# Second block of a two-block model: projections in a new order, sparse attention by pairs of heads, the memory maxima spread by one rounded product per head

## Chip, cores and metric

The kernel runs on one core of one Trainium2 chip. The metric is the device time of one execution in microseconds (us); the time before is the median of three runs, 1567.85 us (1567.51 to 1568.60).

## What is computed

512 tokens of width 1024 go through two different blocks, both in float32. The first block (differential attention, a convolution branch and a feed-forward part) is not touched. The second block is a mixer of three branches over one normalised input, followed by a convolutional feed-forward part:

```python
p = xn @ w_in
mq, mk, mv, mo, mi, mf, lx, lg, aq, ak, av, iq, ik, iw = split_cols(p)
hA = mlstm_chunkwise(mq, mk, mv, mi + b_igate, mf + b_fgate)   # 4 heads of 96
hA = rmsnorm(hA, mlstm_norm) * sigmoid(mo)
xc = causal_depthwise_conv(lx, lru_conv_w, lru_conv_b)
hB = rglru(xc, ...) * gelu(lg)                                 # width 384
hC = dsa_attention(aq, ak, av, iq, ik, iw)                     # 4 heads of 64
return concatenate([hA, hB, hC]) @ w_out
```

`dsa_attention` scores all keys by the index projections (`iq`, `ik`, `iw`), keeps the 128 best keys of each query, and runs a softmax attention of four heads of width 64 over them. `mlstm_chunkwise` is a linear attention whose weights are the exponential of a gate minus a running maximum over the tokens.

## The kernel before

Every large product takes its float32 operands as two rounded parts (type fp32r, high and low), and makes three products of them (high-high, high-low, low-high); `step` (L560) issues these three for one 128-row slice of the contraction, and `units` (L567) runs a unit: one block of 128 output columns over the 8 slices. Weights come in by DMA (`raw`), ACT rounds them (`wh`), and DVE makes the remainder (`wl`).

The order of all instructions is written by the program itself, while it is built: `Build` keeps an estimate of when each tile is ready, and the main thread issues one unit after another in the order of a table; after each `step` a tick (L200) lets background tasks (Python generators) issue what is due by that estimate. So PE's queue holds the units' products with small products of the tasks between them. On the chip every engine works off its own queue in order.

For the mixer of the second block (`block2_mix`, L1434) the table is `UNITS2` (L1355): 23 units that are the column blocks of `w_in`. `'f'` units write features by tokens, `'tok'` units (`av`, `t0`, `t1`, `t2`) tokens by features. `done` (L1795) and `done_tok` (L1837) copy a finished unit out of PSUM and set a flag with its name. `t0` and `t1` hold the values `va` of the memory heads, `t1` and `t2` their output gate `mo`; the last copy of `t2` is followed by two tanh on ACT over all of `mo`.

The tasks are:

- `gates` (L1454): the gates of the memory heads, and the running maximum `self.M` (4 rows, one for each head, by 512 tokens).
- `scores` (L1505): the index scores for the query tiles t = 1, 2, 3, and on DVE 16 rounds of 8 maxima for each tile (48 in all), then the mask `mbs`. They start when `iq1` is done. A score step issues the products of two heads, whose operands lie in partitions 0 to 63 and 64 to 127, behind each other.
- `lrus` (L1547): the recurrence branch, `hc[3]` to `hc[5]`.
- `memory` (L1604), one for each head: spreads the head's row of `self.M` to 128 partitions by a product with a column of the identity (contraction over 4 rows, float32), makes the weights, and sums the values. Two streams of `memories` (L1660) run the heads; they start when `t1` is done. Behind the last head follows one chain: squares on ACT, their sums on DVE, a reciprocal square root in small DVE operations on 16 columns, the scaling of both halves of the result and its product with `mo` on DVE, then on PE three times four transposes, each group read out by ACT and DVE into `hc[0]` to `hc[2]`.
- `sparse` (L1720), 16 steps (t, head): logits by a float32 product with a contraction over 64 rows, for t > 0 the mask added by a bf16 product, the maximum on DVE, the exponential on ACT, transposes on PE, a copy on ACT, the product with `av`, and the division on DVE. Three streams of `sparses` (L1764) run them. `sparse_out` (L1774) makes `hc[6]` and `hc[7]`.

After the table comes the product with `w_out` in 256-column halves. Its first unit (L1938) takes the eight `hc` in the order 3, 4, 5, 0, 1, 2, 6, 7, and goes through seven of them for the first block of columns before it starts the second block. A `hc` that is not there holds everything behind it on PE:

```python
for q, k in enumerate(order[: kt - 1] if len(outs_list) > 1 else order):
    if have:
        self.until(lambda: have(k))
    self.step(outs, ws[u], acts[k], k, q == 0, q == kt - 1)
```

Of the kernel before, what the change touches and what calls it, by code (L numbers as in the profile page):

```python
# [20 lines left out]
SEQ = 512  # L21
# [7 lines left out]
NEG = -1e30  # L29
# [133 lines left out]
class Build:  # L163
# [141 lines left out]
    def mm(self, out, lhsT, rhs, start=True, stop=True):  # L305
        n = free(rhs)
        if rhs.dtype == F32:
            c = max(0.213, n * 4 / 2400)
        elif rhs.dtype == F32R:
            c = max(0.107, n / 2400 + 0.003)  # L310
        else:
            c = max(0.03, n / 2400)
        self.pe_op(c, out, [lhsT, rhs])
        self.nc.tensor.matmul(out, lhsT, rhs, start=start, stop=stop)  # L314

    def tr(self, out, src):
# [922 lines left out]
    def block1_ffn(self):  # L1239
# [114 lines left out]

    UNITS2 = [  # L1355
        ('idx',),
        ('aq0', 'f', 2312),
        ('lg0', 'f', 1928),
        ('aq1', 'f', 2440),
        ('lx0', 'f', 1544),  # L1360
        ('lx1', 'f', 1672),
        ('lx2', 'f', 1800),
        ('iq0', 'f', 3080),
        ('mk0', 'f', 384),
        ('lg1', 'f', 2056),
        ('lg2', 'f', 2184),
        ('iq1', 'f', 3208),
        ('mk1', 'f', 512),
        ('av', 'tok', 2824),
        ('mk2', 'f', 640),  # L1370
        ('mq0', 'f', 0),
        ('mq1', 'f', 128),
        ('t0', 'tok', 768),
        ('mq2', 'f', 256),
        ('t1', 'tok', 1024),
        ('ak0', 'f', 2568),
        ('ak1', 'f', 2696),
        ('t2', 'tok', 1280),
    ]

# [53 lines left out]
    def block2_mix(self):  # L1434
        nc, tc, io, V, S, mm, tr = self.nc, self.tc, self.io, self.V, self.S, self.mm, self.tr
# [6 lines left out]
        with ExitStack() as es:  # L1442
# [3 lines left out]
            B = {}  # L1446
            flags = set()
            hc = [None] * 8
            gt = cst.tile([P, 4, 12], F32, name="gt")
            aa, em, nlf, pre, nF, fg = (g16(n) for n in ("aa", "em", "nlf", "pre", "nF", "fg"))  # L1450
            sp2, spm = cst.tile([P, 3], F32, name="sp2"), cst.tile([P, 3], F32, name="spm")
            wait = lambda f: (0.3 for _ in iter(lambda: f in flags, True))

            def gates():  # L1454
# [26 lines left out]
                for t in range(4):  # L1481
                    tr(pt[0:4, t * P : t * P + P], aa[:, 4 * t : 4 * t + 4])
                yield self.due(pt)
                self.M = B["gT"][0:4]
                V.tensor_copy(self.M, pt[0:4, 0:SEQ])
                self.at_put(i)
                V.tensor_tensor_scan(out=self.M, data0=self.M, data1=self.M, initial=0.0, op0=MAX, op1=MAX)
                yield self.due(self.M)
                i, pt = yield from self.at_get()
                for t in range(4):  # L1490
                    tr(pt[:, 4 * t : 4 * t + 4], self.M[:, t * P : t * P + P])
# [53 lines left out]
            lx = {}  # L1545
# [58 lines left out]
            def memory(h):  # L1604

                i, pt = yield from self.at_get()
                mm(pt[:, 0:512], self.ident[0:4, h : h + 1].to_broadcast([4, P]), self.M)
                yield self.due(pt)
                MB, MBm = halves(self.slot())
                S.activation(MB, pt[:, 0:512], AF.Copy)  # L1610
# [103 lines left out]
                    self.at_put(i)  # L1714
                    hc[c] = x

            STEPS = [(t, h) for t in range(4) for h in range(4)]
            osb, todo, ets = [], list(range(16)), []

            def sparse(n):  # L1720

                t, hd = STEPS[n]
                hp, r64 = hd // 2, slice(64 * (hd % 2), 64 * (hd % 2) + 64)
                yield from wait(f"aq{hp}")
                yield from wait(f"ak{hp}")
                if t:
                    yield from wait(f"mask{t}")
                L = P * (t + 1)
                yield self.due(B["aq"][hp], B["ak"][hp], self.mbs)
                i, pt = yield from self.at_get()  # L1730
                o = pt[:, :L]
                mm(o, B["aq"][hp][r64, t * P : t * P + P], B["ak"][hp][r64, :L], True, t == 0)
                if t:
                    mm(o, self.identb, self.mbs[:, 512 * (t - 1) : 512 * (t - 1) + L], False, True)
                yield self.due(pt)
                if t == 0:
                    V.memset(o[0:64, L - 64 :], NEG)
                nb, l, rl = (self.sm(1, x, bufs=5) for x in ("snb", "sll", "srl"))
                V.tensor_reduce(nb, o, axis=AX.X, op=MAX, negate=True)
                yield self.due(nb)  # L1740
                e = tp.tile([P, 3 + SEQ], F32, name=self.nm("e"), tag="lx", bufs=5)
                S.activation(e[:, :L], o, AF.Exp, bias=nb, accum_out=l)
                self.at_put(i)
                yield self.due(l, e[:, :L])
                i, pt = yield from self.at_get()
                for k in range(t + 1):
                    tr(pt[:, k * P : k * P + P], e[:, k * P : k * P + P])
                yield self.due(pt)
                while not ets:
                    yield 0.1  # L1750
                eT = ets.pop()
                S.activation(eT[:, :L], pt[:, :L], AF.Copy)
                self.at_put(i)
                V.reciprocal(rl, l)
                yield self.due(eT)
                i, pt = yield from self.at_get()
                for k in range(t + 1):
                    mm(pt[:, 0:64], eT[:, k * P : k * P + P], B["av"][:, k, 64 * hd : 64 * hd + 64], k == 0, k == t)
                ets.append(eT)
                yield self.due(pt)  # L1760
                V.tensor_scalar(osb[0][:, t, 64 * hd : 64 * hd + 64], pt[:, 0:64], rl, None, op0=MUL)
                self.at_put(i)

            def sparses():  # L1764
                yield from wait("av")
# [7 lines left out]

            def sparse_out():  # L1774
                for c in range(2):
                    for n in range(16):
                        if STEPS[n][1] // 2 == c:
# [12 lines left out]
                    hc[6 + c] = x  # L1790
# [416 lines left out]
```

## Time and profile before

| | |
|---|---|
| median of three runs | 1567.85 us (1567.51 to 1568.60) |
| the profiled execution, its own time | 1567.5 us |
| its span, first to last instruction | 1565.7 us |
| PE busy | 1546.3 us (99%), 10279 instructions |
| DVE busy | 1101.5 us (70%), 2011 instructions |
| ACT busy | 680.5 us (43%), 1222 instructions |
| mixer of the second block, its stretch of the span | about 928 to 1160 us |

PE multiplies, DVE and ACT work on vectors, POOL fills and gathers, SP issues the weights' DMAs. In a row of the timeline the first number is the start in us from the start of the span, the second the duration; consecutive matmuls overlap, so the cost of one is the distance to the next start (its step), not its duration. A float32 matmul stands as two records, since it is done in two passes. A note in square brackets is the idle time of the engine ahead of the row and what ended it. The granted clock is 1.00 for TensorE's level of 2.4 GHz and 0.50 for that of 1.2 GHz.

### The profile page before, as it was taken

Reading aid. Unit: us, or ns where it says so; the run is one execution under the profiler, and the core shown is the slowest. Engines: PE = TensorE matmul, PEld = TensorE weight load, DVE = VectorE, ACT = ScalarE, POOL = GpSimd, SP = SyncE. Lnnn points to the kernel's source line nnn. Section 1 sums busy time; section 2 is a strip of 40 time slices with the busy share of each in tenths; the row PEclk is TensorE's granted clock in tenths of the full one; section 3 lists DMA queues with packets and bytes.
Section 4 is the critical chain, followed back from the end, with each engine's and each line's share of the span. In section 5 each row is a group of like instructions: output and inputs, shape, how many; then the busy total and the mean of one; then the engine's idle time right before and its main releaser. Section 6 shows DMA issues by size and latency. Waiting matters only on the chain.

```text
span 1565.7 us, 25299 instructions
## 1 busy us (share of the span) xinstructions
PE 1546.3 (99%) x10279; PEld 1386.4 (89%) x10281; DVE 1101.5 (70%) x2011; ACT 680.5 (43%) x1222; POOL 25.9 (2%) x89
## 2 busy tenths in 40 slices
PE   7999999999999999999999999999999999999998
PEld 6999999999999999999988877796799888888886
DVE  4899999997764576776743457899768877775224
ACT  5344544546843343443432223625565544444112
POOL 4000000000000000000000000000000000000000
PEclk9999999999999999999999999999999999999999
DMA  5322222222222333333333332231053133333221
GB/s 145 95 69 75 75 70 80 68 68 68 73 77 71 92 108 93 85 94 95 91 88 98 84 99 80 59 104 55 19 144 109 55 95 95 95 98 102 94 95 68
DMA packets 233005, 134.17 MB, mean 86 GB/s; under 512 B 6925, under 2 KB 228240, under 8 KB 232888
## 3 DMA queue, kind: packets, MB, share of 16 engines
q1 hardware_dynamic: 231448, 130.35, 28.7%
q8 instruction: 81, 1.33, 0.4%
q0 software_dynamic: 1136, 1.15, 0.3%
q10 hardware_dynamic: 304, 1.05, 0.2%
q14 instruction: 36, 0.29, 0.1%
HBM read 130.44 MB, written 2.10 MB: 85 GB/s over the span
## 4 chain that ended last, share of the span: by engine, by line
PE 97%; DVE 1%; ACT 1%; DMA 0%; issue 0%; DVEq 0%; ACTq 0%; POOLq 0%
PE mm L314 70%; PE at L314 24%; PE at L320 3%; ACT act L158 1%; DVE act L158 0%; DMA act<-in_x_dram 0%; DVE yy L158 0%; DVE wl L158 0%; ACT ys L158 0%; DVE yc L158 0%; ACT wh L158 0%; DVE nb L158 0%; DVE fx L158 0%; DVE res L158 0%; ACT e L158 0%
## 5 line engine op out<-in xcount | busy, mean ns | idle before, releaser
L314 PE MATMUL mm<-act,wh 128*128 128x256 f32 (+3 forms) x4720 | 906.2, 306 | 1.5 <-DVE act L158 0.8
L314 PEld LDWEIGHTS mm<-act,wh 128*128 128x128 f32 (+1 forms) x4720 | 692.0, 189 | 49.5 <-issue 10.9
L314 PE MATMUL mm<-act,wl 128*128 128x256 f32 (+4 forms) x2360 | 562.8, 302 | 0.0
L158 ACT ACTIVATE wh<-raw 128x1024 fp32r<-128x1024 f32 (+2 forms) x235 | 245.7, 1047 | 367.5 <-PE mm L314 187.1
L158 DVE TENSOR_TENSOR wl<-raw,wh 128x1024 fp32r<-128x1024 f32 (+2 forms) x235 | 284.5, 1211 | 168.9 <-ACT wh L158 165.9
L314 PEld LDWEIGHTS mm<-act,wl 128*128 128x128 f32 (+1 forms) x2360 | 383.1, 189 | 18.0
L158 DVE SCALAR_TENSOR_TENSOR act<-u,par,act 128x514 f32<-128x514 f32 x232 | 161.1, 748 | 2.2 <-ACT act L158 2.2
L314 PE MATMUL at<-act,wh 128*128 128x512 f32 x416 | 130.3, 394 | 0.0
L314 PEld LDWEIGHTS at<-act,wh 128*128 128x128 f32 x416 | 78.1, 188 | 18.4
L314 PE MATMUL at<-wh,act 128*128 128x512 f32 x264 | 86.0, 395 | 0.0
L314 PE MATMUL mm<-wh,act 128*128 128x256 f32 (+1 forms) x344 | 84.4, 320 | 0.0
L314 PE MATMUL at<-act,act 128*128 128x256 f32 (+9 forms) x468 | 83.5, 329 | 0.8 <-ACT act L158 0.7
L314 PE MATMUL at<-act,wl 128*128 128x512 f32 x208 | 82.0, 394 | 0.0
L158 DVE TENSOR_TENSOR act<-act,act 128x514 f32<-128x514 f32 (+4 forms) x122 | 69.7, 589 | 8.2 <-ACT act L158 7.5
L314 PEld LDWEIGHTS at<-act,act 128*128 128x128 f32 (+1 forms) x468 | 60.2, 189 | 11.1 <-issue 4.7
L158 DVE SCALAR_TENSOR_TENSOR ft<-fx,par,ft 128x512 f32<-128x512 f32 x88 | 65.8, 749 | 1.5
L158 DVE TENSOR_TENSOR fx<-mm,rB 128x514 f32<-128x514 f32 x44 | 30.5, 694 | 50.3 <-PE mm L314 50.1
L314 PEld LDWEIGHTS mm<-wh,act 128*128 128x128 f32 x344 | 57.9, 189 | 7.3 <-issue 3.4
L158 ACT ACTIVATE act<-mm 128x528 f32<-128x528 f32 (+2 forms) x64 | 35.1, 548 | 66.8 <-PE mm L314 66.7
L158 ACT ACTIVATE act<-at 128x128 f32<-128x128 f32 (+6 forms) x88 | 34.4, 413 | 67.8 <-PE at L314 50.2
L158 DVE SCALAR_TENSOR_TENSOR gy<-gx,par,gy 128x512 f32<-128x512 f32 x84 | 62.6, 748 | 1.5
L314 PEld LDWEIGHTS at<-wh,act 128*128 128x128 f32 x264 | 49.6, 188 | 11.6
(286 smaller groups left out, 1435.8 us busy)
## 6 DMA issues: line engine op xcount, KB each, us to landing
raw<-in_w_in_dram SPq DMA_DIRECT2D x82, 512.0 KB, 3.8
raw<-in_w_up_dram SPq DMA_DIRECT2D x44, 512.0 KB, 3.8
raw<-in_ffn_up_dram SPq DMA_DIRECT2D x44, 512.0 KB, 3.9
raw<-in_ffn_down_dram SPq DMA_DIRECT2D x22, 512.0 KB, 3.2
raw<-in_w_out_dram SPq DMA_DIRECT2D x20, 512.0 KB, 3.8
raw<-in_w_down_dram SPq DMA_DIRECT2D x16, 512.0 KB, 3.8
raw<-in_w_conv_out_dram SPq DMA_DIRECT2D x8, 512.0 KB, 3.8
raw<-in_w_down_dram SPq DMA_DIRECT2D x8, 384.0 KB, 3.3
```

The lines of the kernel that those rows point to most:

```text
L158: return f(*a, **k)
L314: self.nc.tensor.matmul(out, lhsT, rhs, start=start, stop=stop)
L320: self.nc.tensor.transpose(out, src, self.ident[p0 : p0 + k, p0 : p0 + k])
```

## The change

Four edits:

1. `UNITS2` gets another order. `iq0` and `iq1` come right behind `idx`, the `mk` units come earlier, `ak0` and `ak1` move from behind `t1` to places ahead of `mq1` and `mq2`. Behind `t1` only `t2` is left, where before `ak0`, `ak1` and `t2` were.
2. `gates` also builds `self.ML`, a tile of 64 rows of type fp32r that is zero but for rows 0 to 3 (the rounded running maximum) and rows 32 to 35 (the remainder), and `self.sel`, which adds the two.
3. `memory` spreads its row by one fp32r product over these 64 rows in place of the float32 product over 4 rows.
4. A step of `sparse` takes two heads: both logits are issued behind each other, then both masks, and then the rest of each head in turn. There are 8 steps, and two streams in place of three.

```diff
     UNITS2 = [
         ('idx',),
+        ('iq0', 'f', 3080),
+        ('iq1', 'f', 3208),
         ('aq0', 'f', 2312),
-        ('lg0', 'f', 1928),
-        ('aq1', 'f', 2440),
         ('lx0', 'f', 1544),
         ('lx1', 'f', 1672),
         ('lx2', 'f', 1800),
-        ('iq0', 'f', 3080),
+        ('lg0', 'f', 1928),
         ('mk0', 'f', 384),
+        ('aq1', 'f', 2440),
+        ('mk1', 'f', 512),
         ('lg1', 'f', 2056),
+        ('mk2', 'f', 640),
         ('lg2', 'f', 2184),
-        ('iq1', 'f', 3208),
-        ('mk1', 'f', 512),
         ('av', 'tok', 2824),
-        ('mk2', 'f', 640),
         ('mq0', 'f', 0),
+        ('ak0', 'f', 2568),
         ('mq1', 'f', 128),
         ('t0', 'tok', 768),
+        ('ak1', 'f', 2696),
         ('mq2', 'f', 256),
         ('t1', 'tok', 1024),
-        ('ak0', 'f', 2568),
-        ('ak1', 'f', 2696),
         ('t2', 'tok', 1280),
     ]
...
+            self.sel = cst.tile([64, 4], F32R, name="sel")
...
-                self.M = B["gT"][0:4]
+                self.M, ML = B["gT"][0:4], self.slot(F32R)[0:64, 0, :SEQ]
+                zero = self.ident[0:64, None, :].to_broadcast([64, 4, P])
+                V.tensor_scalar(ML.rearrange("p (t n) -> p t n", n=P), zero, 0.0, None, op0=MUL)
+                V.tensor_tensor(self.sel, self.ident[0:64, 0:4], self.ident[0:64, 32:36], op=ADD)
...
                 yield self.due(self.M)
+                S.activation(ML[0:4], self.M, AF.Copy)
+                yield self.due(ML)
+                tt(ML[32:36], self.M, ML[0:4].bitcast(F32), SUB)
+                self.ML = ML
...
-                mm(pt[:, 0:512], self.ident[0:4, h : h + 1].to_broadcast([4, P]), self.M)
+                mm(pt[:, 0:512], self.sel[:, h : h + 1].to_broadcast([64, P]), self.ML)
...
-            STEPS = [(t, h) for t in range(4) for h in range(4)]
-            osb, todo, ets = [], list(range(16)), []
+            STEPS = [(t, hp) for t in range(4) for hp in range(2)]
+            osb, todo, ets = [], list(range(8)), []
...
-                i, pt = yield from self.at_get()
-                o = pt[:, :L]
-                mm(o, B["aq"][hp][r64, t * P : t * P + P], B["ak"][hp][r64, :L], True, t == 0)
+                ats = []
+                for _ in range(2):
+                    ats.append((yield from self.at_get()))
+                for q, (_, pt) in enumerate(ats):
+                    r64 = slice(64 * q, 64 * q + 64)
+                    mm(pt[:, :L], B["aq"][hp][r64, t * P : t * P + P], B["ak"][hp][r64, :L], True, t == 0)
                 if t:
-                    mm(o, self.identb, self.mbs[:, 512 * (t - 1) : 512 * (t - 1) + L], False, True)
+                    for _, pt in ats:
+                        mm(pt[:, :L], self.identb, self.mbs[:, 512 * (t - 1) : 512 * (t - 1) + L], False, True)
...
-            for _ in range(3):
+            for _ in range(2):
                 self.start(sparses(), 0.0)
```

Since the tasks issue their work where it is due, the whole mixer is issued in another order. Three places follow.

PE, the last query tile of the sparse attention (t = 3; `at` are its PSUM tiles, `act_1313` and `act_1174` the queries and keys of two heads, `sel` the selector of the memory heads). Before, one head with its mask:

```order
L314 MATMUL at_1521_11936<-act_1369_11334,act_1173_10107 128x512
L314 LDWEIGHTS identb_114
L314 MATMUL at_1521_11936<-mbs_9890,identb_114 128x512
L314 MATMUL at_1522_11939<-act_1259_10631,act_1277_10762 128x64 x4
L314 MATMUL at_1523_11944<-act_1259_10631,act_1277_10762 128x64 x4
```

Now:

```order
L314 MATMUL at_1481_11703<-act_1211_10300,sel_9882 128x512
L314 MATMUL at_1482_11705<-act_1313_10932,act_1174_10111 128x512
L314 MATMUL at_1483_11706<-act_1313_10932,act_1174_10111 128x512
L314 LDWEIGHTS identb_114
L314 MATMUL at_1482_11705<-mbs_9891,identb_114 128x512
L314 LDWEIGHTS identb_114
L314 MATMUL at_1483_11706<-mbs_9891,identb_114 128x512
```

The two heads' logits stand behind each other, and the product that spreads a memory maximum reads `sel`. In the order of before, logits from different halves of the partitions are neighbours at two places among the 16: two heads of t = 0, and a head of t = 0 with one of t = 1.

PE, from the last product of the last unit `t2` to the transposes of the memory branch (`at<-ident`, from the finished halves of the result), and on. Before (`mm_1395` is `t2`, `mm_1510` the first block of `w_out`, `e_` the exponentials of the sparse attention, `act_1515` and `act_1518` the halves):

```order
L314 MATMUL mm_1395_11436<-wh_1372_11342,act_1142_9857 128x256
L320 MATMUL at_1506_11879<-ident_109,e_1501_11865 128x128 x3
L314 MATMUL mm_1510_11889<-act_1266_10700,wh_1397_11442 128x256 x2
L314 MATMUL mm_1510_11889<-act_1266_10700,wl_1398_11443 128x256
L320 MATMUL at_1516_11904<-ident_109,e_1505_11874 128x128 x4
L314 MATMUL mm_1510_11889<-act_1279_10769,wh_1397_11442 128x256 x2
L314 MATMUL mm_1510_11889<-act_1279_10769,wl_1398_11443 128x256
L314 MATMUL mm_1510_11889<-act_1287_10810,wh_1397_11442 128x256 x2
L314 MATMUL mm_1510_11889<-act_1287_10810,wl_1398_11443 128x256
L314 MATMUL at_1519_11924<-act_1259_10631,act_1277_10762 128x64 x3
L320 MATMUL at_1520_11928<-ident_109,e_1517_11909 128x128 x4
```

The first transposes of the halves (`at_1527`) stand 6 rows behind these, and more sparse work stands behind them. Now (`mm_1451` is `t2`, `mm_1530` the first block of `w_out`, `act_1543` and `act_1544` the halves, `act_1546` is `hc[0]`):

```order
L314 MATMUL mm_1451_11551<-wh_1453_11554,act_1142_9857 128x256
L314 MATMUL mm_1530_11959<-act_1285_10755,wh_1464_11583 128x256 x2
L314 MATMUL mm_1530_11959<-act_1285_10755,wl_1465_11584 128x256
L314 MATMUL mm_1530_11959<-act_1287_10784,wh_1464_11583 128x256 x2
L314 MATMUL mm_1530_11959<-act_1287_10784,wl_1465_11584 128x256
L314 MATMUL mm_1530_11959<-act_1290_10819,wh_1464_11583 128x256 x2
L314 MATMUL mm_1530_11959<-act_1290_10819,wl_1465_11584 128x256
L320 MATMUL at_1545_12021<-ident_109,act_1543_12012 128x128 x2
L320 MATMUL at_1545_12021<-ident_109,act_1544_12016 128x128 x2
L320 MATMUL at_1547_12029<-ident_109,act_1543_12012 128x128 x2
L320 MATMUL at_1547_12029<-ident_109,act_1544_12016 128x128 x2
L314 MATMUL mm_1530_11959<-act_1546_12026,wh_1464_11583 128x256 x2
```

All of the sparse attention stands ahead of the end of `t2`; between that end and the transposes there are the nine products of `hc[3]` to `hc[5]`.

ACT, the same place. Now, from the copy of the last memory head's sums (`at_1522`) on (`mm_1451` is the last copy of `t2`, `act_1277` and `act_1479` are `mo`, `act_1535` and `act_1536` the squares):

```order
L158 ACTIVATE act_1455_11556<-at_1522_11901 128x2x97
L158 ACTIVATE act_1456_11557<-at_1522_11901 128x2x97
L158 ACTIVATE act_1479_11667<-mm_1451_11551,R_9868 128x256
L158 ACTIVATE act_1277_10697<-act_1277_10697 128x512
L158 ACTIVATE act_1479_11667<-act_1479_11667 128x1024
L158 ACTIVATE act_1535_11972<-act_1455_11556 128x768
L158 ACTIVATE wh_1533_11966<-raw_1452_11552 128x1024
L158 ACTIVATE act_1536_11983<-act_1456_11557 128x768
L158 ACTIVATE wh_1538_11988<-raw_1463_11581 128x1024
L158 ACTIVATE act_1546_12026<-at_1545_12021,wn_9918 128x512
```

Before, the two squares stood 7 and 4 rows ahead of the last copy of `t2`, with the tanh behind it; now they stand behind both. On DVE, the remainder `wl` of the second `w_out` unit stands between the sums of the first and the second square.

## Rows read from the trace of the kernel before

**Rows 1.** The page, busy time of each engine.
```profile
PE 1546.3 (99%) x10279; PEld 1386.4 (89%) x10281; DVE 1101.5 (70%) x2011; ACT 680.5 (43%) x1222; POOL 25.9 (2%) x89
```

**Rows 2.** Busy us of PE, PEld, DVE, ACT, POOL in the mixer's last stretch.
```profile
1124.50:1143.50 19.00, 17.51 (x132) 14.87 (x131) 11.91 (x25) 12.12 (x24) 0.20 (x2) 1.00 0.20 56
```

**Rows 3.** Timeline of PE, the last wait of that stretch.
```profile
1143.50 0.50 PE L314 MATMUL mm<-act,wh 128*128 128x256 f32 x2 [0.48 <-ACT act L158]
```

**Rows 4.** Timeline of PE: index scores, then logits; start, duration, operation, records.
```profile
1007.87 1.13 PE L314 MATMUL at<-act,act 64*128 64x512 f32 x4
1008.93 0.39 PE L314 MATMUL mm<-wh,act 128*128 128x256 f32 x1
...
1084.45 0.70 PE L314 MATMUL at<-act,act 64*128 64x128 f32 x4
...
1121.83 0.28 PE L314 MATMUL mm<-wh,act 128*128 128x256 f32 x1
1122.04 1.12 PE L314 MATMUL at<-act,act 64*128 64x512 f32 x2
1123.10 0.39 PE L314 MATMUL at<-mbs,identb 128*128 128x512 bf16 x1
...
1123.91 0.40 PE L314 MATMUL mm<-wh,act 128*128 128x256 f32 x2
```

**Rows 5.** Timeline of PE: the spreading of one memory head's maximum.
```profile
1085.72 1.12 PE L314 MATMUL at<-act,ident 4*128 4x512 f32 x2
1086.77 0.39 PE L314 MATMUL mm<-wh,act 128*128 128x256 f32 x1
```

**Rows 6.** Groups of PE by shape, 928 to 1160 us: busy us, mean ns of one.
```profile
L314 PE MATMUL mm<-act,wl 128*128 128x512 f32 x120 | 47.3, 394 | 0.0
```

**Rows 7.** Timeline of PE, the last product of `t2`, and of ACT around it.
```profile
1124.27 0.28 PE L314 MATMUL mm<-wh,act 128*128 128x256 f32 x1
...
1116.35 0.84 ACT L158 ACTIVATE act<-act 128x768 f32<-128x768 f32 x1
...
1124.59 0.47 ACT L158 ACTIVATE act<-mm,R 128x256 f32<-128x256 f32 x1 [0.97 <-PE mm L314]
1124.96 1.57 ACT L158 ACTIVATE act<-act 128x512 f32<-128x512 f32 x2
...
1129.36 1.08 ACT L158 ACTIVATE wh<-raw 128x1024 fp32r<-128x1024 f32 x1
1131.88 0.69 ACT L158 ACTIVATE act<-at,wn 128x512 fp32r<-128x512 f32 x1 [1.43 <-PE at L320]
```

**Rows 8.** Timeline of DVE, the memory branch's chain.
```profile
1117.22 0.95 DVE L158 TENSOR_REDUCE sumsq<-act 128x8 f32<-128x768 f32 x1
1118.09 0.17 DVE L158 TENSOR_TENSOR den<-den,em 128x16 f32<-128x16 f32 x1
...
1121.51 0.17 DVE L158 TENSOR_TENSOR rd<-rd,rsy 128x16 f32<-128x16 f32 x1
...
1127.25 0.94 DVE L158 TENSOR_TENSOR act<-act,rd 128x768 f32<-128x768 f32 x1
1128.22 1.03 DVE L158 SCALAR_TENSOR_TENSOR act<-act,act 128x256 f32<-128x256 f32 x2
...
1129.49 1.21 DVE L158 TENSOR_TENSOR wl<-raw,wh 128x1024 fp32r<-128x1024 f32 x1
...
1132.77 0.74 DVE L158 SCALAR_TENSOR_TENSOR act<-at,wn,act 128x512 fp32r<-128x512 f32 x1
```

**Rows 9.** Timeline of PE near both ends, and the last window's granted clock (before DMA share).
```profile
5.40 1.09 PE L320 MATMUL mm<-ident,act 128*128 128x128 f32 x4 [2.56 <-DMA act<-in_x_dram]
...
24.36 0.76 PE L320 MATMUL at<-ident,act 128*128 128x128 f32 x5
...
1558.53 0.39 PE L314 MATMUL mm<-wh,act 128*128 128x512 f32 x1
...
1564.00:1566.00 2.00, 0.00 (x0) 0.00 (x0) 0.00 (x0) 0.00 (x0) 0.00 (x0) 0.50 0.16 59
```

More of the change, by code (lines that the diff above doesn't have):

```diff
@@ L1715, in memories @@
                     hc[c] = x
-            STEPS = [(t, h) for t in range(4) for h in range(4)]
-            osb, todo, ets = [], list(range(16)), []
+            STEPS = [(t, hp) for t in range(4) for hp in range(2)]
+            osb, todo, ets = [], list(range(8)), []
             def sparse(n):
-                t, hd = STEPS[n]
-                hp, r64 = hd // 2, slice(64 * (hd % 2), 64 * (hd % 2) + 64)
+                t, hp = STEPS[n]
                 yield from wait(f"aq{hp}")
@@ L1729, in sparse @@
                 yield self.due(B["aq"][hp], B["ak"][hp], self.mbs)
-                i, pt = yield from self.at_get()
-                o = pt[:, :L]
-                mm(o, B["aq"][hp][r64, t * P : t * P + P], B["ak"][hp][r64, :L], True, t == 0)
-                if t:
-                    mm(o, self.identb, self.mbs[:, 512 * (t - 1) : 512 * (t - 1) + L], False, True)
[L1735 to L1762, printed above, removed]
+                ats = []
[4 more added lines that the diff above has]
+                    mm(pt[:, :L], B["aq"][hp][r64, t * P : t * P + P], B["ak"][hp][r64, :L], True, t == 0)
@@ new lines, in sparse @@
+                if t:
+                    for _, pt in ats:
+                        mm(pt[:, :L], self.identb, self.mbs[:, 512 * (t - 1) : 512 * (t - 1) + L], False, True)
+                es = []
+                for i, pt in ats:
+                    o = pt[:, :L]
+                    yield self.due(pt)
+                    if t == 0:
+                        V.memset(o[0:64, L - 64 :], NEG)
+                    nb, l = (self.sm(1, x, bufs=5) for x in ("snb", "sll"))
+                    V.tensor_reduce(nb, o, axis=AX.X, op=MAX, negate=True)
+                    yield self.due(nb)
+                    e = tp.tile([P, 3 + SEQ], F32, name=self.nm("e"), tag="lx", bufs=5)
+                    S.activation(e[:, :L], o, AF.Exp, bias=nb, accum_out=l)
+                    self.at_put(i)
+                    es.append((e, l))
@@ new lines, in sparse @@
+                for q, (e, l) in enumerate(es):
+                    hd, rl = 2 * hp + q, self.sm(1, "srl", bufs=5)
+                    yield self.due(l, e[:, :L])
+                    i, pt = yield from self.at_get()
+                    for k in range(t + 1):
+                        tr(pt[:, k * P : k * P + P], e[:, k * P : k * P + P])
+                    yield self.due(pt)
+                    while not ets:
+                        yield 0.1
+                    eT = ets.pop()
+                    S.activation(eT[:, :L], pt[:, :L], AF.Copy)
+                    self.at_put(i)
+                    V.reciprocal(rl, l)
+                    yield self.due(eT)
+                    i, pt = yield from self.at_get()
+                    for k in range(t + 1):
+                        mm(pt[:, 0:64], eT[:, k * P : k * P + P], B["av"][:, k, 64 * hd : 64 * hd + 64], k == 0, k == t)
+                    ets.append(eT)
+                    yield self.due(pt)
+                    V.tensor_scalar(osb[0][:, t, 64 * hd : 64 * hd + 64], pt[:, 0:64], rl, None, op0=MUL)
+                    self.at_put(i)
@@ L1775, in sparse_out @@
                 for c in range(2):
-                    for n in range(16):
-                        if STEPS[n][1] // 2 == c:
+                    for n in range(8):
+                        if STEPS[n][1] == c:
                             yield from wait(f"sp{n}")
```

## The prediction

> **What bounds the kernel now.** I read the page's busy times first: PE is busy for 1546.3 of 1565.7 us [rows 1], so what the change takes off PE's queue or adds to PE's waits is the time, and the other engines matter only where PE waits for them. The second view is the table of stretches: in the mixer's last 19.00 us PE is busy for 17.51, so it waits 1.49 us there [rows 2]; one wait of 0.48 us is for the copies of the first `w_out` block [rows 3], which stays. Ahead of that stretch the mixer's PE waits next to nothing. Third comes the timeline of PE, for what each small product costs: its step to the next start. Last come the timelines of ACT and DVE around the end of the unit `t2`, because the new order leaves something uncovered there.
>
> **Logits by pairs.** The index scores already show what a pair costs: two heads at 512 columns, four records, start at 1007.87, and the next product at 1008.93, 1.06 us for both [rows 4]. One head alone takes 1.06 us as well (1122.04 to 1123.10). So the second head is free, since the two use different halves of the partitions. A step is some 0.06 below the duration: 0.64 us at 256 columns (1084.45, where a head of t = 0 rides along), and midway, 0.85, at 384. Before, t = 1, 2, 3 each pay four times; now twice. That is 2 x (0.64 + 0.85 + 1.06) = 5.1 us. For t = 0 nothing changes: one pair, one rider and one alone before, two pairs now. Entering a 64-row product costs extra: the product ahead of it takes 0.21 us (1121.83 to 1122.04), where 0.12 is usual (0.40 for two less 0.28 for one) [rows 4]. Fourteen entries become eight: 0.5 us. Together **-5.6 us**; ends -4.5 (no entry saved, pairs a little apart) and -6.
>
> **Spreading the maxima.** Four products of 1.05 us each (1085.72 to 1086.77) [rows 5], in two float32 passes. One fp32r pass of 512 columns has a mean duration of 0.394 us [rows 6], a step of 0.23. The new product also enters and leaves a 64-row form, so its cost lies between 0.23 and half of the old one, 0.53; I take 0.33, near the row of its own type. 4 x 0.72 = **-2.9 us**; ends -2.1 and -3.3. Building `ML` and `sel` adds three DVE instructions and one on ACT in the chain of the gates, well ahead of its first reader (which waits for `t1`); PE has units to do there, so I cost it at nothing. If that cover were gone it would be about 2 us, four operations at about the 0.47 to 0.69 us of ACT rows of this size [rows 7].
>
> **The order itself** adds or removes no large product and no DMA; each queue has the same transfers. Scores and rounds of maxima come earlier, so all of the sparse attention ends ahead of `t2`'s end. The small waits in the last stretch go with it: 1.49 - 0.48 = **-1.0 us**. Up to here the gains are 9.5 us.
>
> **What is late next: the chain of the memory branch.** It starts when `t1` is done. Before, `ak0`, `ak1`, `t2` and half of the sparse attention lay behind that; now only `t2` does. Between the end of `t2` and the transposes of the halves PE's queue holds nine products, 9 x 0.12 = 1.1 us, and PE works in order. Count from the end of `t2`'s last product, z = 1124.27 + 0.28 in the trace of before [rows 7].
>
> ACT: the copy starts at z + 0.04 (1124.59) and the tanh at z + 0.41 (1124.96); they end at z + 2.0, and the first square, now queued behind them, runs from about z + 1.9 to 2.75 (0.84). A rounding of weights follows (1.08, to 3.75), and then the second square, to 4.5 [rows 7]. DVE: the sum of the first square, then the remainder `wl` (1.21), which waits for the rounding and ends at z + 4.9; behind it the second sum, step 0.87 (1117.22 to 1118.09), to 5.8 [rows 8]. The small operations step through 3.4 us (1118.09 to 1121.51) and 0.2 for the last: z + 9.4. Each half of the result takes 2.0 us (1127.25 to the end of 1128.22 + 1.03): z + 11.4 and **z + 13.3**.
>
> PE restarts there. The first group's last two transposes need 0.2, and 0.3 to come out; ACT takes 0.69 (the row at 1131.88) and DVE 0.74 (1132.77): `hc[0]` is whole at z + 15.3, `hc[1]` by DVE's queue at 15.9, and `hc[2]`, whose transposes stand behind the products of `hc[0]`, at 17.6. With its last products PE is through at z + 17.8. The work done in that time, 18 products at 0.12 and 12 transposes at 0.11, is 3.4 us, begun 0.2 us ahead of z. So PE loses 17.8 + 0.2 - 3.4 = **+14.6 us**. Ends: 12 if the remainder `wl` doesn't delay the second sum and the transposes of the first half start the rest early; 17 if the last head's copies are late as well.
>
> **The clock.** After PE's last product at 1558.53 the granted clock is 0.50, the 1.2 GHz level, in the window 1564 to 1566 [rows 9]; the new gap, from z + 0.9 to z + 11.4, is 10.5 us, longer than that. At the program's start four transposes take 1.09 us, 0.22 apart; at 24.36 five take 0.76, 0.12 apart [rows 9]. At the slow step the transposes and products of the restart add 1.2 us to the chain above, and I let six more products pass slowly, 0.7 us: **+1.9 us**, a choice, since no row here shows a gap in mid-program; ends 0 and 3.
>
> The Trainium skill (TensorE: Matmul & The Clock Gate, section "Why this matters for your kernels") warns of idle gaps between bursts of matmuls in mid-kernel, because TensorE goes back to half its clock. It speaks against this change, which buys fewer PE cycles with a gap; rows 9 agree for the program's end. By the rule the sum is the one below, without it 1.9 us less.
>
> **Sum.** The profiled execution took 1567.5 us. 1567.5 - 5.6 - 2.9 - 1.0 + 14.6 + 1.9 = 1574.5. The median of the three runs lies 0.35 us above the profiled one, so I forecast 1574.9 us, 0.45% slower.
>
> **Rivals.** A measurement of this kernel can tell a difference of about 0.2%, 3.1 us, from none.
>
> 1. *Faster: the chain is covered.* PE saves its 9.5 us and the gap doesn't open: 1567.85 - 9.5 = 1558.4. For it: PE's share of 99% [rows 1], so whatever PE saves shows at once; and before, the same chain cost PE next to nothing. The point that decides: the time from `t2`'s end to the halves, which has to stay below the 1.1 us of products queued there; with a loss under 9.5 - 3.1 = 6.4 us it would still be measurably faster. Against: the two squares stand behind the tanh in ACT's order, and 5.8 us of DVE's and ACT's rows lie between them and the small operations alone. Chance 0.11.
> 2. *Half of it.* If DVE and ACT go through the tail faster than before's rows, a loss of 6.4 to 12.6 us and no slow clock leaves the time within 0.2%: 1564.7 to 1571.0. Chance 0.09.
> 3. *The clock stays up*: 1573.0. For it: 10.5 us is not far above what rows 9 show. Chance 0.14.
> 4. *A starved middle.* Index scores and 48 rounds come earlier, where DVE must also make each unit's `wl` of 1.21 us; PE would wait at unit starts, 1 to 4 us more: 1576 to 1579. Against: DVE has 30% free over the span [rows 1]. Chance 0.10.
> 5. *The change doesn't do what it says on PE*: masks or PSUM keep the pair's products apart, or the fp32r product over 64 rows costs what the old one did; 8.5 us of the gain are lost at most, about 1580. Against: the pairs of the index scores. Chance 0.05.
>
> **How the numbers follow.** The forecast, 1573.5 to 1576.5, gets 0.51. Slower by over 0.2% are the forecast and rivals 3, 4 and 5: 0.51 + 0.14 + 0.10 + 0.05 = 0.80. Within 0.2% is rival 2, 0.09; faster is rival 1, 0.11. The range for 8 in 10 goes from 1569.7 (gains whole, the loss 12 us and no slow clock, 1567.85 - 10.2 + 12) to 1578.8 (gains 7.5, loss 15.5, clock 3: 1567.85 + 11); it takes in the forecast, rival 3, most of rival 4 and the upper part of rival 2, and leaves out rivals 1 and 5.
>
> **What would show it.** In the profile after: two logits of equal length starting within 0.01 us of each other, 1.06 us for a pair at 512 columns; the spreading product as one record with a step near 0.33; PE's busy time down by some 9 us; a new wait of PE for DVE of about 10 us near 1130 to 1140, with the transposes of the halves behind it; the tanh ahead of the squares on ACT; and a granted clock of 0.50 somewhere behind that gap. I am wrong if PE shows no wait of over 5 us there, or if the squares or the last copy of the memory heads turn out to be done well ahead of `t2`.

## The result, and the profile after

| | before | after |
|---|---|---|
| median | 1568.22 us (1567.51 to 1569.81, 4 runs) | 1577.26 us (1576.52 to 1577.71, 4 runs) |
| span of the profiled execution | 1565.7 us | 1575.3 us |

The ratio is 1.0056, interval 1.0040 to 1.0072: 0.56% slower, where 0.45% was forecast. (Of all the runs in this document one execution, 4180.94 us in the last experiment, stands apart from its ten neighbours and is left out of the ratio there.) PE's busy time shrank all the same, by 3.3 us. The page's busy times of after, against [rows 1]:

```profile
PE 1543.0 (98%) x10276; PEld 1387.1 (88%) x10277; DVE 1100.1 (70%) x2014; ACT 680.9 (43%) x1223; POOL 25.8 (2%) x89
```

What became of the logits and of the spreading stands in the groups of PE by shape from 928 to 1180 us (busy us, mean ns of one). Before (index scores of the same shapes are in the groups, alike in both kernels):

```profile
L314 PE MATMUL at<-act,act 64*128 64x512 f32 x16 | 6.7, 641 | 0.0
L314 PE MATMUL at<-act,act 64*128 64x384 f32 x16 | 5.5, 535 | 0.0
L314 PE MATMUL at<-act,ident 4*128 4x512 f32 x8 | 4.5, 639 | 0.0
L314 PE MATMUL at<-act,act 64*128 64x256 f32 x16 | 4.2, 428 | 0.0
L314 PE MATMUL at<-act,act 64*128 64x128 f32 x8 | 1.5, 322 | 0.0
```

After:

```profile
L314 PE MATMUL at<-act,act 64*128 64x512 f32 x16 | 4.7, 634 | 0.1
L314 PE MATMUL at<-act,act 64*128 64x384 f32 x16 | 3.7, 535 | 0.0
L314 PE MATMUL at<-act,act 64*128 64x256 f32 x16 | 2.8, 428 | 0.0
L314 PE MATMUL at<-act,sel 64*128 64x512 f32 x4 | 2.0, 495 | 0.0
L314 PE MATMUL at<-act,act 64*128 64x128 f32 x8 | 1.0, 323 | 0.0
```

The logits' numbers of records are the same, and the mean of one is nearly so, but busy time counts what overlaps once: the logits fall from 17.9 to 12.2 us, by 5.7, and the spreading from 4.5 to 2.0, by 2.5. Now the other side, the two largest of PE's waits of after (us in total, times, longest) in the same stretch:

```profile
PE at L320 <- DVE act L158: 11.0, 2, 9.7
PE mm L314 <- DVE act L158: 1.5, 3, 0.9
```

The 9.7 us are the gap behind `t2`. PE's timeline of after around it:

```profile
1127.95 0.28 PE L314 MATMUL mm<-wh,act 128*128 128x256 f32 x1
...
1129.02 0.28 PE L314 MATMUL mm<-act,wl 128*128 128x256 f32 x1
1139.01 0.69 PE L320 MATMUL at<-ident,act 128*128 128x128 f32 x2 [9.71 <-DVE act L158]
1140.94 1.54 PE L320 MATMUL at<-ident,act 128*128 128x128 f32 x6 [1.24 <-DVE act L158]
...
1143.34 0.58 PE L314 MATMUL mm<-act,wh 128*128 128x256 f32 x1 [0.35 <-DVE act L158]
...
1146.56 0.58 PE L314 MATMUL mm<-act,wh 128*128 128x256 f32 x1 [0.20 <-DVE act L158]
...
1152.65 0.51 PE L314 MATMUL mm<-act,wh 128*128 128x256 f32 x2 [0.48 <-ACT act L158]
```

The first row is the last product of `t2`, so z = 1127.95 + 0.28 = 1128.23; then come the nine products of `hc[3]` to `hc[5]`, nothing for 9.7 us, and the transposes of the first half. The chain that they wait for, on ACT and DVE of after (compare [rows 7, 8]):

```profile
1128.64 2.29 ACT L158 ACTIVATE act<-act 128x512 f32<-128x512 f32 x3
```

```profile
1131.91 1.22 DVE L158 TENSOR_TENSOR wl<-raw,wh 128x1024 fp32r<-128x1024 f32 x1
1133.06 0.95 DVE L158 TENSOR_REDUCE sumsq<-act 128x8 f32<-128x768 f32 x1
...
1137.33 0.17 DVE L158 TENSOR_TENSOR rd<-rd,rsy 128x16 f32<-128x16 f32 x1
1137.54 0.96 DVE L158 TENSOR_TENSOR act<-act,rd 128x768 f32<-128x768 f32 x1
...
1140.46 1.03 DVE L158 SCALAR_TENSOR_TENSOR act<-act,act 128x256 f32<-128x256 f32 x2
```

The two tanh and the first square are one row of three on ACT; the remainder `wl` stands ahead of the second sum on DVE; the small operations end at z + 9.3 and the second half at 1141.49, z + 13.3. The granted clock by stretches of after (start and end, length, the busy us of PE, PEld, DVE, ACT and POOL, then the clock as the third number from the end):

```profile
1130.00:1135.00 5.00, 0.00 (x0) 0.00 (x0) 3.89 (x9) 3.56 (x5) 0.00 (x0) 0.80 0.09 24
...
1145.00:1150.00 5.00, 4.66 (x20) 4.07 (x20) 0.75 (x1) 0.69 (x1) 0.00 (x0) 0.50 0.15 44
1150.00:1155.00 5.00, 4.51 (x37) 4.31 (x37) 0.78 (x1) 3.15 (x6) 0.00 (x0) 0.99 0.00 0
```

It falls to the 1.2 GHz level (0.50) within the gap and is still there from 1145 to 1150, where PE has its products again; it is back in the stretch from 1150 on.

### The profile page after: what moved, and what is told of

Read it like the earlier page. It is cut to its first block, busy times and chain, and to the rows that moved or that the text cites. A ratio compares the mean times of both kernels' runs of the same rounds, so it can differ in the third digit from the quotient of the medians.

```text
span 1575.3 us, 25296 instructions
## 1 busy us (share of the span) xinstructions
PE 1543.0 (98%) x10276; PEld 1387.1 (88%) x10277; DVE 1100.1 (70%) x2014; ACT 680.9 (43%) x1223; POOL 25.8 (2%) x89
## 4 chain that ended last, share of the span: by engine, by line
PE 95%; DVE 2%; ACT 1%; issue 1%; DMA 0%; DVEq 0%; ACTq 0%; POOLq 0%
PE mm L314 69%; PE at L314 24%; PE at L320 3%; DVE act L158 1%; ACT act L158 1%; DMA act<-in_x_dram 0%; DVE wl L158 0%; DVE yy L158 0%; DVE rsa L158 0%; DVE sumsq L158 0%; ACT ys L158 0%; DVE yc L158 0%; DVE res L158 0%; DVE rsy L158 0%; DVE nb L158 0%
## 5 line engine op out<-in xcount | busy, mean ns | idle before, releaser
L314 PE MATMUL mm<-wh,act 128*128 128x256 f32 (+1 forms) x344 | 88.7, 325 | 0.9 <-DVE act L158 0.9
L314 PE MATMUL at<-act,act 128*128 128x256 f32 (+8 forms) x468 | 78.7, 329 | 0.3 <-ACT act L158 0.2
L158 DVE TENSOR_TENSOR act<-act,act 128x514 f32<-128x514 f32 (+5 forms) x123 | 70.4, 591 | 8.2 <-ACT act L158 7.6
L320 PE MATMUL at<-ident,act 128*128 128x128 f32 (+6 forms) x298 | 47.0, 277 | 13.7 <-DVE act L158 13.7
```

What stands on the lines that cost most here:

```text
L158: return f(*a, **k)
```

## The experiments

**The order of before under the rest of the change.** Only the table `UNITS2` is put back, so that it ends as before:

```diff
...
-        ('ak0', 'f', 2568),
         ('mq1', 'f', 128),
         ('t0', 'tok', 768),
-        ('ak1', 'f', 2696),
         ('mq2', 'f', 256),
         ('t1', 'tok', 1024),
+        ('ak0', 'f', 2568),
+        ('ak1', 'f', 2696),
         ('t2', 'tok', 1280),
```

> The changed kernel with the order of the units as before (pairs of heads, the spreading product and two streams stay). Theory (the order uncovers the memory branch's chain): the gap of some 10 us is gone, most of the gains of 9.5 us are left, but pairs end late now, with waits of 2 to 5 us in the last stretch: 1560 to 1565 us. Rival (the pairs, not the order, make the loss, since two streams take longer through the tail): 1574 us or more.

Measured: 1570.92 us, ratio 1.0017 (1.0008 to 1.0026): a miss. The gap of 10 us is gone, but the gains are not there. PE's timeline:

```profile
1113.70 1.50 PE L314 MATMUL at<-act,act 128*128 128x64 f32 x8 [1.02 <-ACT act L158]
...
1121.60 0.58 PE L314 MATMUL mm<-act,wh 128*128 128x256 f32 x1 [3.12 <-DVE act L158]
```

With `ak0` and `ak1` late, nearly all sparse attention stands in the tail. What the pairs save there is work that lay over the memory chain and over the sparse steps' own copies: PE now waits for both, 7.3 us in all from 928 to 1180, where before has 1.4. Behind the 3.12 us wait the granted clock falls too (0.61 in 1120 to 1125). Against the spreading alone (1565.43 us, below), which has the same order, the pairs in two streams cost 5.5 us here in place of a gain. Which of the two brings the waits, the pairs or the two streams in place of three, is not shown: no run has the one without the other.

**The order alone.** The kernel before, with the new table; its diff is the first hunk of the change.

> The kernel of before with the new order of the units alone. Theory: the whole loss without the gains: one wait of PE of about 10 us, a slow clock behind it, about 17 us lost at the end and 1 to 2 in the middle, 1 us of old waits saved: 1583 to 1588 us. Rival (the pairs make the loss): within 3 us of before, 1568.

Measured: 1587.24 us, ratio 1.0120 (1.0106 to 1.0134), as expected. The same gap, with no gains against it; it is 1.4 us longer than in after, since one more rounding `wh` (1.04 us on ACT) and its remainder `wl` (1.23 us on DVE) stand ahead of the first square and its sum:

```profile
1149.97 0.69 PE L320 MATMUL at<-ident,act 128*128 128x128 f32 x2 [11.07 <-DVE act L158]
```

**The spreading alone.** The kernel before, with `ML`, `sel` and the fp32r product; its diff is the change's parts in `gates` and `memory`, of which the last is:

```diff
-                mm(pt[:, 0:512], self.ident[0:4, h : h + 1].to_broadcast([4, P]), self.M)
+                mm(pt[:, 0:512], self.sel[:, h : h + 1].to_broadcast([64, P]), self.ML)
```

> The kernel of before with the spreading of the memory maxima by the fp32r product alone. In the profile after, the product has a step of 0.43 us where the float32 one had 1.05: 4 x 0.62 = 2.5 us less, 1565.7. Rival (the small product is hidden or the extra work in the gates' chain shows): no change, 1568.

Measured: 1565.43 us, ratio 0.9982 (0.9973 to 0.9991), as expected: this part gains its 2.5 us (1568.2 less 2.8), and building the two tiles costs nothing that can be seen.

**The gap filled.** After, with 42 products whose output nobody reads, ahead of the first `hc` that is not there:

```diff
+def there(k):
+    if hc[k] is None and not idle:
+        i, pt = self.at_now()
+        idle.append(i)
+        for _ in range(42):
+            nc.tensor.matmul(pt, hc[3][:, 0, 0:P], hc[3][:, 0, 0:SEQ], start=True, stop=True)
+        self.at_put(i)
+    return hc[k] is not None
...
```

> The changed kernel with 42 additional matmuls of 512 columns on PE, whose result nobody reads, placed where PE waits for the memory branch (about 9.7 us of PE work in the wait of 10.4). They only keep PE busy. Theory (the slow clock costs 2 to 3 us of the loss): the granted clock stays at 1.00, the time falls to 1574 to 1575 us. Rival (the chain alone counts, the clock behind it nothing): 1577. Rival (the added matmuls delay the chain): above 1577.

Measured: 1577.35 us, ratio 1.0058 (1.0045 to 1.0071); no gain. The windows show why this did not measure the clock:

```profile
1138.00:1142.00 4.00, 2.09 (x12) 1.03 (x10) 3.93 (x7) 0.76 (x2) 0.00 (x0) 1.00 0.00 0
1142.00:1144.00 2.00, 1.20 (x5) 1.00 (x6) 1.77 (x3) 0.53 (x1) 0.00 (x0) 0.81 0.11 34
1144.00:1150.00 6.00, 5.66 (x25) 5.07 (x24) 0.75 (x1) 0.69 (x1) 0.00 (x0) 0.50 0.26 76
```

The clock held through the filled gap and then fell in the thin work behind it, where PE is half idle, so the dense products from 1144 on still passed at 0.50.

**The squares ahead of the tanh.** After, with the tanh taken out of `done_tok` and put behind the squares in `memories`:

```diff
                 yield from wait("mo")
+                for x in B["mo"]:
+                    S.activation(x, x, AF.Tanh, scale=0.5)
+                yield self.due(*B["mo"])
```

> The changed kernel, but the two tanh over `mo` are issued behind the squares (ACT's order is then: last copy of `t2`, first square, rounding of `w_out`, second square, tanh). If the chain ACT squares, DVE sums, small operations, halves is what PE waits for, all of it moves forward by the two tanh's step of 1.5 us: 1575.8 us, and PE's wait falls from 9.7 to some 8.2 us. Rival: the remainder `wl` of the second `w_out` unit or the copy of the memory sums sets the chain; then nothing moves, 1577.3 us.

Measured: 1577.19 us, ratio 1.0058 (1.0041 to 1.0074): a miss, but not for the rival's reason. DVE's timeline:

```profile
1136.02 0.18 DVE L158 TENSOR_TENSOR rd<-rd,rsy 128x16 f32<-128x16 f32 x1
1136.13 1.23 DVE L158 TENSOR_TENSOR wl<-raw,wh 128x1024 fp32r<-128x1024 f32 x1
1137.27 0.95 DVE L158 TENSOR_TENSOR act<-act,rd 128x768 f32<-128x768 f32 x1
```

The small operations do end 1.3 us earlier (1137.33 in after). But the remainder of the third `w_out` unit, which stood behind the halves, now stands ahead of them and takes 1.0 us of it back: the halves start at 1137.27, in after at 1137.54, and PE still waits 9.36 us.

**A fill with work that is needed.** After, with `w_out` begun as two units of 512 columns over `hc` 3 to 7:

```diff
-    js = [0, 1] if half + j == 0 else [j]
+    if j == 0:
+        ps = [self.mm_ps()[:, :SEQ] for q in range(2)]
+        self.units([[(o, SEQ, 0)] for o in ps], hc, ..., order=[3, 4, 5, 6, 7, 0, 1, 2], first=5)
+        continue
```

> The changed kernel, but `w_out` begins with both first column blocks at 512 columns over the five `hc` that are there (3 to 7), and only then asks for `hc` 0 to 2; the same products in all. Behind `t2` stand then 30 products at 0.23 = 6.9 us of work that is needed anyway, in place of 1.1 us. If the loss is PE without work, 5.8 us come back: 1571.5 us, and down to 1569 if the granted clock stays at 1.00 as well. Rival (what the filled gap suggests: filling does not shorten what follows): 1575 to 1577, with slow products behind the wait, or the second half's fewer products uncover the first half's norm.

Measured: 1570.58 us, ratio 1.0014 (1.0005 to 1.0024). Of the 1577.3 us 6.7 came back, as expected: the 5.8 of PE's time and 0.9 more. That the 0.9 is the clock's is not shown; the granted clock still falls to 0.50 here (1140 to 1148), and the weights of these two blocks are rounded once in this run, where after does it for each half. What the chain holds up is PE, and mainly for want of work.

**The key units late.** After, with the last hunk of the first experiment alone: `ak0` and `ak1` stand behind `t1` again, and the rest of the table is the new one.

> The changed kernel with `ak0` and `ak1` behind `t1`, as before the change, and the rest of the new order kept. If the place of these two units alone uncovers the memory chain, the gap goes and the gains of 9.5 us are left: 1559 to 1562 us. Rival, from the run with the old order: with `ak` late all sparse steps stand in the tail, two streams of pairs do not keep PE busy there, and the time is about that run's, 1569 to 1572 us.

Measured: 1572.30 us, ratio 1.0028 (1.0018 to 1.0038): the rival's case, 0.3 us above its range. The place of these two units does uncover the chain, since the longest wait is now 2.0 us; but putting them back moves all sparse steps into the tail, and the waits take another form, 8.2 us in all from 928 to 1180, as with the old order.

**The chain shortened, alone and with the fill.** The squares first, and in `weights` the units of `w_out` from the third on wait until both halves are issued:

```diff
-            while i >= self.gate:
+            while i >= self.gate or i >= self.held:
                 yield 0.2
```

> The changed kernel with the squares ahead of the tanh, and with the weights of `w_out` from the third unit on held back until the halves are issued, so that no third remainder `wl` slips in between the small operations and the halves. Chain theory: 1.5 us from the tanh and 1.1 us from `wl`; PE's wait for the first half about 7.0 to 7.5 us, the time 1574.6 us. Rival: something else of DVE or ACT takes the free place again, or the third unit's weights are late for PE; 1576.5 to 1578 us.

Measured: 1576.03 us, ratio 1.0052 (1.0037 to 1.0067). PE's wait is shorter by the tanh alone:

```profile
1138.49 0.69 PE L320 MATMUL at<-ident,act 128*128 128x128 f32 x2 [8.33 <-DVE act L158]
```

9.71 - 8.33 = 1.4 us. My 2.6 counted `wl` twice: in after the third one stood behind the halves anyway. So the chain is what PE waits for, and the move was worth 1.4 of the wait. The time is 1.2 us below after, 0.9 when each is taken against its own runs of before; the two intervals overlap, so that the trace shows the gain and the time alone does not.

> Both: the first two column blocks at 512 columns over the five finished `hc` first, squares ahead of the tanh, weights held back. The fill left two waits of 2.5 and 2.4 us and a granted clock of 0.50 from some 1138 to 1148. If 2.6 us go from the chain, 1568.0 us; if with shorter waits the granted clock also stays at 1.00, 1566.5 us. Rival: the chain is no longer the bound, the weights are; 1570 to 1571 us.

Measured: 1568.53 us, ratio 1.0004 (0.9995 to 1.0014), the same as before the change; 2.0 us less than the fill alone (1.6 when each is taken against its own runs of before) where 2.6 was expected, and with the granted clock still at 0.50 from 1140 to 1145.

**The clock's price.** The filled gap again, and 13 more unread products in the waits behind it, the first six so:

```diff
                     for t in range(4):
+                        if c == 0 and t == 2:
+                            j, dt = yield from self.at_get()
+                            for _ in range(6):
+                                nc.tensor.matmul(dt, hc[3][:, 0, 0:P], hc[3][:, 0, 0:SEQ], start=True, stop=True)
+                            self.at_put(j)
                         tr(pt[:, t * P : t * P + P], ha[t // 2][:, t % 2, c * P : c * P + P])
```

> The changed kernel with the gap filled as in the run before with 42 unread products of 512 columns, and with 13 more of them in the short waits behind it: 6 between the transposes of the first and of the second half, 4 ahead of the products of `hc[0]`, 3 ahead of those of `hc[2]`. Every result that the first products wait for still comes at its own time. If the slow clock behind the gap costs what I forecast (1.9 us), the granted clock stays at 1.00 and the time is 1575.0 to 1575.8 us. Rival: the clock has no price beside the chain's, 1577.3 us; or the extra products themselves hold up PE, over 1577.5 us.

Measured: 1574.92 us, ratio 1.0044 (1.0027 to 1.0060), 2.3 us less than after (2.0 when each is taken against its own runs of before). PE's timeline and the granted clock:

```profile
1143.44 0.39 PE L314 MATMUL mm<-act,wh 128*128 128x256 f32 x1 [0.32 <-DVE act L158]
...
1145.95 0.39 PE L314 MATMUL mm<-act,wh 128*128 128x256 f32 x1 [0.40 <-DVE act L158]
...
1150.50 0.51 PE L314 MATMUL mm<-act,wh 128*128 128x256 f32 x2 [0.48 <-ACT act L158]
```

```profile
1144.00:1146.00 2.00, 1.60 (x12) 1.20 (x10) 0.79 (x2) 0.69 (x1) 0.00 (x0) 1.00 0.82 240
```

With z at 1128.30 here, `hc[0]` is whole at z + 15.1 as in after, the products of `hc[2]` go on at z + 17.7 (after: z + 18.3), and those behind them pass at the fast step up to the next unit (1150.50).

**Two other orders.** The kernel with chain and fill, with the table in these two orders:

```
idx iq0 mk0 lg0 lx0 iq1 mq0 lg1 lg2 lx1 aq0 mk1 av mk2 t0 mq1 lx2 ak0 mq2 t1 ak1 aq1 t2
idx iq0 lx0 mq0 lx1 aq0 mq1 lg0 mq2 mk0 iq1 t0 lg1 av lx2 mk1 mk2 lg2 ak0 t1 ak1 aq1 t2
```

> The kernel of the run before with chain and fill (1568.5 us), in another order: only `iq0` of the two `iq` early, `t1` followed by `ak1`, `aq1` and `t2`, so that the chain of the memory branch starts two units of 5.6 us earlier against the end of `t2`. That run still waits 1.4 us in the middle and 4.3 us in the tail, and its products behind the waits pass at a granted clock of 0.50 for some 6 us (about 2.5 us lost). If the distance from `t1` to the end of the table is what decides, nearly all of that goes: 1560.5 to 1562.5 us, faster than before the change. Rival: the second pair of heads, whose keys now come late, stands in the tail instead, as with the old order: 1566 to 1571 us.

> As the run beside it, with another table of the same kind: the `mq` and `iq1` in other places, `t1` again followed by `ak1`, `aq1` and `t2`. The tail should go the same way, 1560.5 to 1562.5 us, and the difference between the two shows what the middle of the mixer costs; with the second pair of heads standing in the tail 1566 to 1571 us.

Measured: 1565.80 us, ratio 0.9986 (0.9977 to 0.9995), and 1564.78 us, ratio 0.9980 (0.9971 to 0.9989). Both are a little faster than before the change by their intervals, by 2.2 and 3.2 us, and both miss the 1560.5 to 1562.5 that I expected. The second one's waits from 928 to 1175 us:

```profile
PE at L314 <- ACT act L158: 1.8, 3, 0.7
PE at L314 <- DVE act L158: 1.3, 1, 1.3
PE mm L314 <- ACT act L158: 0.7, 1, 0.7
PE mm L314 <- DVE act L158: 0.4, 2, 0.2
```

No gap is left, and the granted clock stays at 1.00 through the tail. The waits are 4.2 us; without them it would be 1560.6 us. Of these, 2.9 us are in the tail, the part of the rival that came true: three are for the copies of the second pair's sparse steps, which now stand there, and three are for the two parts of `hc[6]` and `hc[7]`, which are the sparse attention's result. The wait of [rows 3], for the first `w_out` copies, is gone. The other 1.3 us are lost in the middle (1075.09), where a small product of a background task waits for DVE, which has rounds of maxima ahead. The best version is not measurably faster than the spreading alone (0.9982).

## Why the prediction was right

The measured 1577.26 us lies in the stated range but above the forecast's own 1573.5 to 1576.5, where rival 4 stood. By the prediction's own steps, in us:

| step | forecast | measured in after |
|---|---|---|
| logits by pairs | -5.6 | -5.7 (groups by shape) |
| spreading | -2.9 | -2.5 |
| small waits of the last stretch | -1.0 | -1.0 (none left ahead of the gap) |
| chain of the memory branch | +14.6 | +14.9 |
| clock | +1.9 | +2.2 |
| waits in the middle | 0 (a rival) | +1.6 |
| sum | +7.0 | +9.5 (spans: 1575.3 - 1565.7 = 9.6) |

*Pairs.* Two logits of 512 columns and the mask behind them, in after's timeline:

```profile
1100.52 1.13 PE L314 MATMUL at<-act,act 64*128 64x512 f32 x4
1101.59 0.60 PE L314 MATMUL at<-mbs,identb 128*128 128x512 bf16 x2
```

1.07 us for both heads. That the index scores' pairs were the right model is shown. That the sum agrees to 0.1 us is partly chance: the groups fall by 5.2 us at 256 to 512 columns, where 5.1 was forecast, and by 0.5 at 128 columns, where nothing was; there a head stood as busy before that rode along with another one and cost PE nothing ([rows 4], 1084.45). The 0.5 forecast for the entries is not in these groups.

*Spreading.* The step mis-sized: 0.43 us in place of the 0.33 I took between 0.23 and 0.53.

```profile
1084.94 0.50 PE L314 MATMUL at<-act,sel 64*128 64x512 f32 x1
1085.37 0.39 PE L314 MATMUL mm<-wh,act 128*128 128x256 f32 x1
...
1098.70 0.49 PE L314 MATMUL at<-act,sel 64*128 64x512 f32 x1
1098.71 1.34 PE L314 MATMUL at<-act,act 64*128 64x512 f32 x4
1099.99 0.39 PE L314 MATMUL at<-mbs,identb 128*128 128x512 bf16 x1
```

4 x 0.62 = 2.5 (the fourth, at 1098.70, saves a little more). I leaned on the row of the same type and undersized the change between forms. The logits' steps in after are 0.42, 0.63, 0.84 and 1.06 us at 128, 256, 384 and 512 columns, which is 0.21 for each 128 columns and 0.21 besides; and where a pair of logits follows the spreading product at once (1098.70 to 1099.99), both take 1.29, some 0.22 more than the pair alone. So by an estimate from these rows the product itself costs about 0.22, as the row of its own type, and 0.21 is paid once for a run of 64-row products.

*The chain.* Forecast against measured, counted from z: small operations 9.4 and 9.3, second half 13.3 and 13.3, `hc[0]` whole 15.3 and 15.1, `hc[2]` 17.6 and 18.3 (17.7 with the fast clock). The first two transposes began at z + 10.8 and not at 11.4, which gained nothing, as the others wait for the second half. From the first of the nine products (1128.07) to the next unit (1152.65) pass 24.6 us; 48 products at 0.118, 12 transposes at 0.11 and the 0.48 wait are 7.5. The loss is 17.1, of which 2.2 is the clock's, so 14.9. That the order opens the gap is shown by the order alone (+19 us on the kernel before), that PE mainly lacks work in it by the useful fill (-6.7), that ACT's and DVE's order sets its length by the squares' place (-1.4 of the wait).

One sign failed: PE's busy time was to fall by some 9 us and fell by 3.3 (1546.3 to 1543.0). Of the 17.1 us only 11.5 stand as waits (9.71, 1.24, 0.35 and 0.20); the other 5.6 stand as busy, among them the products at the slow step and the ends of products with nothing behind them.

*The clock.* The run kept busy took the next unit to z + 22.2 (1150.50 less 1128.30), after to z + 24.4: 2.2 us, where 1.9 was chosen. Its parts were sized the wrong way round, so the sum is near by luck: 1.2 us was put into the chain and 0.7 behind it, and measured are 0.6 up to the products of `hc[2]` (z + 18.3 against 17.7) and 1.6 behind them. The price is less than a sixth of the chain's 14.9. In the gap of 9.71 us the granted clock went from 1.00 to 0.50; the sentence of the Trainium skill (TensorE: Matmul & The Clock Gate, "Why this matters for your kernels") that idle gaps in mid-kernel bring TensorE back to half its clock agrees with this.

*The middle.* Here I costed nothing, and it is the largest part of the 2.4 us by which I was low. It is rival 4 at its lower end, alongside the forecast rather than in its place: PE is busy for 98.42 us from 1000 to 1100, before for 99.98. In after's timeline two products of `tok` units wait:

```profile
1007.84 0.38 PE L314 MATMUL mm<-wl,act 128*128 128x256 f32 x1 [0.52 <-DVE wl L158]
...
1010.28 0.39 PE L314 MATMUL mm<-wh,act 128*128 128x256 f32 x1 [0.90 <-DVE act L158]
```

A third, of 0.17 us, is for a copy of ACT at 1082.55. DVE at the two waits:

```profile
1005.44 1.22 DVE L158 TENSOR_TENSOR_SCAN act<-act 128x512 f32<-128x512 f32 x1
1006.58 1.20 DVE L158 TENSOR_TENSOR wl<-raw,wh 128x1024 fp32r<-128x1024 f32 x1
...
1008.42 1.22 DVE L158 TENSOR_TENSOR_SCAN act<-act 128x512 f32<-128x512 f32 x1
1009.56 0.66 DVE L158 TENSOR_TENSOR act<-mm,rB 128x512 f32<-128x512 f32 x1
```

DVE comes late with a remainder and with the copy that frees a PSUM tile, as the rival said, but not for the rival's reason: ahead of both stand scans of the recurrence branch (`lrus`), and the next round of maxima starts only at 1011.88. DVE's share does not tell the two kernels apart, neither the 30% that I held against the rival nor the one of this stretch: from 1000 to 1100 DVE is busy for 92.36 us in after and for 93.25 in before, where PE does not wait. What counts is which work stands ahead in DVE's queue. The 0.90 us wait is also in the run with the order alone, so the order brings it; the 0.52 us wait is not, and what brings it is open.

Rivals 1 and 2 fell with the 9.7 us wait, rival 3 with the granted clock, rival 5 with the groups by shape. Two slips of the prediction do not touch its sum: with 8.5 us of gain lost rival 5 comes to 1583.4 us and not to about 1580, and the 5.8 us in rival 1 count from the end of `t2`, not from the squares.

## What to carry to other kernels

Where a scheduler's table decides the order, look for the chain that the last unit covers, write down each engine's queue from that unit's end, and count to the moment at which PE can go on; the work that PE loses is not a gain as long as it was cover. A shorter chain can be filled by whatever stands next in the same engine's queue (here a weight remainder of 1.2 us), so the queue has to be read again after each move. Useful products that are ready, put ahead of those that aren't, gave back more here than the repair of the chain.

## What was not expected of the hardware

- A product of 64 rows in fp32r at 512 columns takes a step of 0.43 us when a product of 128 rows follows, nearly twice the 0.23 of 128 rows in the same type (42 of them in 9.70 us in the filled gap), but adds only some 0.22 to a pair of 64-row products that follows it. Two float32 products of 64 rows side by side take 1.07, as one does.
- In an otherwise filled gap the granted clock stayed at 1.00 until the half-idle work behind it (2.09 us busy of 4.00, then 0.81 and 0.50): to hold it, the short waits had to be filled too, and then no stretch of the tail showed less than 1.00. The profile's granted clock stands at 1.00 in the program's first 20 us too, although the transposes of [rows 9] are 0.22 us apart there, as the six of after are at 0.50 (1140.94, 1.54 us): at a start it has to be read with the steps beside it.
